# Block differences of h in the index stage's score buffers, spread over the second half of the token stage

## The chip, the cores and the metric

The kernel runs on one core of a Trainium2 chip. The metric is the device time of one execution in microseconds. Three runs of the kernel before took 2882.2, 2875.97 and 2873.57 us; the median is 2875.97 us. The profile shown here is of one more execution, which took 2868.78 us.

## The reference

One step of a one-layer streaming encoder: a normalised, modulated input `h` is projected by one wide matrix, and its columns feed a sparse attention with an indexer, a gated short convolution, and merge gates.

```python
h = rms_norm(x, norm_g) * (1.0 + scale[:, None, :]) + shift[:, None, :]
proj = h @ w_in                     # 9,000-odd columns, split into
(q, k, v, za, qi, ki, wi, u, bg, cg, zb, ga, gb) = jnp.split(...)
...
logits = einsum('bqhd,bsd->bqhs', qi, ki) * IDX_DIM ** -0.5
score  = einsum('bqh,bqhs->bqs', wi * IDX_HEADS ** -0.5, relu(logits))
_, idx = lax.top_k(score, 256)      # then attention over the gathered keys
...
y = x + gate * (merged @ w_out)
```

There are 2048 prompt tokens and 32 sample tokens, 1024 model channels, 8 index heads of 64 channels.

## The kernel before

**Number format.** Every large product is made of three fast matmuls: an operand is split into a high part (a cast) and a low part (operand minus high part), and high x high, low x high and high x low are added up in PSUM.

**Token stage** (lines 492 to 901). `h` is made tile by tile (`mk_h`, line 633): a tile of x is normalised, transposed on TensorE, scaled into `f`, split into `hhi` and `hlo`, and `f` is stored to the DRAM tensor `h_d` (line 649), channels by tokens. From it come the columns i0 and i1 (index queries and keys), k and v: for each tile of 128 tokens and each column group, 24 matmuls (`chunk`, lines 760 to 762) into one of 5 PSUM banks `pm`. The copies out of PSUM go into 5 buffers `sm`, are turned or normalised on VectorE and stored. The tokens are done in two halves (8 tiles, then 9 with the sample tokens). `tok_steps` (line 740) gives a list of steps for a half: in the second half steps 0 to 22 are i0 and i1 with the making of `h` for later pairs of tiles (steps 4, 9, 14), step 23 prepares weights, steps 24 to 32 are k, steps 33 to 41 are v.

**Block differences.** The next stage multiplies `h` by the feature weights with seven products of half-size blocks in place of eight. It needs four differences of the four blocks of `h` (two halves of the channels by two halves of the tokens); they are kept in the DRAM tensor `t_d`. For a chunk of 352 (or 336) tokens and a pair of channel tiles kt and kt+4, `sums_load` (line 659) loads two tiles x from `h_d` (line 662, both token halves in one tile), and `block_sums` (line 664) makes four subtractions on VectorE (line 671) and stores both tiles to `t_d` (line 673). There are 12 such differences: 3 chunks by 4 values of kt. Their tiles come from `xtile`, the four buffers of tag x in pool `xp`, which also hold the raw x of `mk_h`. In the list of steps, the load of a difference stands at step 15 and every fourth position after it, its subtractions three positions later, and the next load right behind those.

**Feature stage, pass 0** (from line 903). Its pools lie over the SBUF space of the token stage's pools: the tiles `ev` through which operands come in (7 buffers) begin where `xp` began; the weight tiles `wr` (line 925), `ws` and `wo` lie over the token stage's weights, and most of the operand tiles `bh` and `bl` over `hhi` and `hlo`. `b_piece` (line 966) loads four tiles `ev` (line 974) from `h_d` or `t_d`, splits each into `bh` (ScalarE, line 190) and `bl` (VectorE, line 191). Pass 0 needs 9 such pieces, 36 loads: three pieces of `h_d`, then six of `t_d`. `mm` (line 982) then makes 12 matmuls a piece (lines 988 to 990).

**Index stage.** Woven between the products run the index scores (`index_steps`, line 213): transposes (line 237), two matmuls per 512 (or 352) keys and head (lines 246 and 247), relu on ScalarE (line 248), scaled sum on VectorE into a score tile `sc` (lines 250 and 252; two buffers of 8 KB a partition in pool `ip`), then a bisection for the threshold. The first block is the sample's (block 16, 32 tokens), then 15, 14, ...

**Order.** A scheduler orders the instructions of each engine ahead of time from the order in which the code emits them, their priorities and its own estimates; it may bring index work forward. Loads and stores, but for a few, are issued from one queue, SyncE's (SP), in that order: a DMA that waits there holds all behind it. `tc.keep_in_program_order` fixes the order of the loads and subtractions of the differences among themselves.

Of the kernel before, what the change touches and what calls it, by code (L numbers as in the profile page):

```python
# [9 lines left out]
F32 = mybir.dt.float32  # L10
# [9 lines left out]
P = 128  # L20
D = 1024
KT = 8
SEQ = 2048
# [5 lines left out]
HT = NTOK // 2  # L29
# [35 lines left out]
TCOLS = _o  # L65


class Env:
    def __init__(self, **kw):
        self.__dict__.update(kw)  # L70
# [31 lines left out]

@with_exitstack
def body(ctx, tc, x_prompt, x_sample, cache_k, cache_v, cache_idx_k, state_conv, c_prompt, c_sample,
         w_ada, w_g, b_ada, norm_g, w_t, w_f, q_norm_g, k_norm_g, conv_w, w_q, rope, turns, ident_in, rows_in,
         y_p, y_s, k_p, v_p, ki_p, conv_p, k_s, v_s, ki_s, conv_s):
    nc = tc.nc
    V, S, G, T = nc.vector, nc.scalar, nc.gpsimd, nc.tensor
    load = nc.sync.dma_start
# [4 lines left out]
    def nm(s):  # L114
        uid[0] += 1
        return f"{s}_{uid[0]}"
# [35 lines left out]
    ident = cp.tile([P, P], F32, name="ident")  # L152
# [7 lines left out]
    heads = cp.tile([P, 8], F32, name="heads")  # L160
# [328 lines left out]
    ip = pix.enter_context(tc.tile_pool(name="ip", bufs=1))  # L489
# [17 lines left out]
    with ExitStack() as p1:  # L507
# [9 lines left out]
        def xtile():  # L517
            return xp.tile([P, D], F32, name=nm("x"), tag="x", bufs=4)
# [134 lines left out]
        halved = {}  # L653
# [3 lines left out]
            return x[:, :2 * tb].rearrange("p (h t) -> p h t", h=2), d.rearrange("p (h t) -> p h t", h=2)[:, :, c0:c0 + tb]  # L657

        def sums_load(ch, kt):
            xs = halved[ch, kt] = xtile(), xtile()  # L660
            for x, k in zip(xs, (kt, kt + 4)):
                tc.keep_in_program_order(load(*both(x, h_d[k], *CHUNKS[ch])))

        def block_sums(ch, kt):

            c0, tb = CHUNKS[ch]
            x1, x2 = halved.pop((ch, kt))
            a, b = slice(0, tb), slice(tb, 2 * tb)
            for o, p, q in ((x1[:, a], x1[:, b], x1[:, a]), (x1[:, b], x2[:, b], x1[:, b]),
                            (x2[:, b], x2[:, b], x1[:, a]), (x2[:, a], x2[:, a], x2[:, b])):  # L670
                tc.keep_in_program_order(V.tensor_tensor(o, p, q, ALU.subtract))
            for x, k in ((x1, kt), (x2, kt + 4)):
                store(*both(x, t_d[k], c0, tb)[::-1])
# [64 lines left out]
        def tok_steps(tiles, pairs, w0, p0, first):  # L738

            pend = []
            steps = []

            def flush():
                now = pend[:]
                pend.clear()
                for f in now:
                    f()

            def chunk(pi, ti):
                kind, cols = TOK[pi]
                hi, lo = wspl[w0 + pi]
                ncol = sum(w for _, w in cols)
                t, n, off = tiles[ti]
                r0 = t * P
                pm = acc()
                for kt in range(KT):
                    a, b_ = hhi[:, kt, off:off + n], hlo[:, kt, off:off + n]
                    T.matmul(pm[:n, :ncol], a, hi[:, kt, :ncol], start=(kt == 0), stop=False)  # L760
                    T.matmul(pm[:n, :ncol], a, lo[:, kt, :ncol], start=False, stop=False)
                    T.matmul(pm[:n, :ncol], b_, hi[:, kt, :ncol], start=False, stop=(kt == KT - 1))
                flush()
                if ti == 1 and pi > 1:
                    w_ahead(w0 + pi)
                if kind == "k":
                    sq = norm_stage1(pm, n)

                    def fin():
                        qn = norm_stage2(pm, sq, gk, t, n)  # L770
                        dst = (k_p[0, r0:r0 + n] if t < NB else k_s[0]).rearrange("t h d -> t (h d)")
                        store(dst, qn[:n, :256])
                        store(k_d[r0:r0 + n, :], qn[:n, :256])
                    pend.append(fin)
                elif kind == "v":
                    vs = small()
                    S.copy(vs[:n, :256], pm[:n, :256])
                    S.dma_start((v_p[0, r0:r0 + n] if t < NB else v_s[0]).rearrange("t h d -> t (h d)"), vs[:n, :256])
                    S.dma_start(v_d[r0:r0 + n, :], vs[:n, :256])
                elif kind == "i0":  # L780
                    vs = small()
                    S.copy(vs[:n, :264], pm[:n, :264])

                    def fin():
                        V.tensor_copy(wi[:n, t, :], vs[:n, 256:264])
                        rope_apply(vs[:n, :256].rearrange("p (h d) -> p h d", h=4), 4, 16, t, n)
                        store(qi_d[r0:r0 + n, 0:256], vs[:n, :256])
                    pend.append(fin)
                else:
                    vs = small()  # L790
                    S.copy(vs[:n, :320], pm[:n, :320])

                    def fin():
                        rope_apply(vs[:n, :320].rearrange("p (h d) -> p h d", h=5), 5, 16, t, n)
                        store(qi_d[r0:r0 + n, 256:512], vs[:n, :256])
                        store(ki_p[0, r0:r0 + n] if t < NB else ki_s[0], vs[:n, 256:320])
                        store(ki_d[r0:r0 + n, :], vs[:n, 256:320])
                        if t < NB:
                            pend.append(idx_key(env, kiT, r0, vs[:n, 256:320], n))
                        else:  # L800
                            pend.append(idx_key(env, kiS, PAST, vs[:n, 256:320], n))
                    pend.append(fin)

            def pair_ahead(i):
                if i + 2 < len(pairs):
                    mk_h(p0 + i + 2)
                if i == 1:
                    w_load(w0 + 2)

            for i, pr in enumerate(pairs):  # L810
                for pi in range(2):
                    for ti in range(2 * i, 2 * i + len(pr)):
                        steps.append((1.0, lambda pi=pi, ti=ti: chunk(pi, ti)))
                steps.append((0.3, lambda i=i: pair_ahead(i)))

            def third():
                w_split(w0 + 2)
                w_load(w0 + 3)

            steps.append((0.1, third))  # L820
            for pi in range(2, nw):
                for ti in range(len(tiles)):
                    steps.append((1.0, lambda pi=pi, ti=ti: chunk(pi, ti)))
            if first:
                for j in range(2):
                    at = len(steps) - (len(tiles) - 4 - 3 * j)
                    steps.insert(at, (0.3, lambda j=j: mk_h(p0 + len(pairs) + j)))
            else:
                at = 15
                for j in range(12):  # L830
                    ch, kt = j // 4, j % 4
                    steps.insert(at, (0.0, lambda ch=ch, kt=kt: sums_load(ch, kt)))
                    steps.insert(at + 3, (0.1, lambda ch=ch, kt=kt: block_sums(ch, kt)))
                    at += 4
            steps.append((0.1, flush))
            return steps

# [52 lines left out]
    with ExitStack() as p2:  # L890
# [183 lines left out]
        def turns_load(hf, ch):  # L1074

            c0, tb = CHUNKS[ch]
            turned[ch] = ev(), ev()
            for a, t in enumerate(turned[ch]):
                load(t[:, :tb], turns[a, :, hf * HT + c0:hf * HT + c0 + tb])

        def query(ct, f, hf, ch, uu, ps, second):

# [792 lines left out]
def _consts():  # L1875
    pos = np.concatenate([np.arange(SEQ), PAST + np.arange(NS)]).astype(np.float32)
    cols = []
    for rot in (32, 16):
        hf = rot // 2
        inv = np.float32(500000.0) ** (np.float32(-2.0) * np.arange(hf, dtype=np.float32) / np.float32(rot))  # L1880
        ang = (pos[:, None] * inv[None, :].astype(np.float32)).astype(np.float32).astype(np.float64)
        cols += [np.cos(ang), np.sin(ang)]
    table = np.concatenate(cols, axis=1).astype(np.float32)
    rows = np.zeros(32, np.float32)
    rows[0:ROUNDS + 1] = 0.5 ** np.arange(ROUNDS + 1)
    rows[16:24] = np.arange(1, 9)
    table = np.concatenate([table, np.zeros((17 * P - NTOK, 48), np.float32)]).reshape(17, P, 48).transpose(1, 0, 2).reshape(P, 17 * 48)
    turns = np.stack([np.tile(t.T, (8, 1)) for t in cols[:2]]).astype(np.float32)
    heads = np.kron(np.eye(8), np.ones((16, 1)))
    return {"rope": table, "turns": turns, "ident": np.concatenate([np.eye(P), heads], axis=1).astype(np.float32), "rows": rows}  # L1890


def _chunks(w):
# [59 lines left out]
```

## Time and profile before

| what | value |
|---|---|
| profiled execution, its own time | 2868.78 us |
| its span, first to last instruction | 2867.0 us |
| median of three runs | 2875.97 us |
| TensorE (PE) matmuls, busy | 2749.5 us, 18206 |
| VectorE (DVE) busy | 2193.7 us, 4549 instructions |
| ScalarE (ACT) busy | 1508.4 us, 2719 instructions |
| GpSimd (POOL) busy | 1049.3 us, 1430 instructions |
| mean granted TensorE clock | 0.984 |

The token stage's second half begins at about 150 us of the span; its last matmul starts at 270.99 us. The page of a profile lists busy time per engine, then the span in 40 slices of 71.7 us, in which each digit is a busy share (or the granted clock) in tenths. Other views used below are stages (busy time in chosen stretches, with the granted clock, the busy share of the DMA engines and GB/s behind it), groups of instructions by line and shape, the timeline of an engine or queue in order of time, and who waited for whom.

### The profile page before, as it was taken

To read this page: it belongs to the slowest core of one execution; us is meant where nothing else is said; L and a number is where in the kernel's file an instruction comes from. 1 tells how busy PE (TensorE), PEld (TensorE's weight loads), DVE (VectorE), ACT (ScalarE), POOL (GpSimd) and SP (SyncE) were. 2 spreads that over 40 slices of the span, in tenths; PEclk is the share of its full clock that TensorE was granted. 3 is DMA by queue.
4 is the path that set the end of the run, shared out by engine and by line. 5 is a ranking of instruction groups with operands and counts; after the bars stand their busy time and mean duration, and the time that the engine had idled before them with its cause. 6 is when DMAs were issued, how large, how long until landed. Compare 5 with 4: busy or idle time off the path is not lost. (4 is left out here: it accounts for less than half of the span.)

```text
span 2867.0 us, 51829 instructions
## 1 busy us (share of the span) xinstructions
PE 2749.5 (96%) x18206; PEld 2642.5 (92%) x18206; DVE 2193.7 (77%) x4549; ACT 1508.4 (53%) x2719; POOL 1049.3 (37%) x1430
## 2 busy tenths in 40 slices
PE   8998699999999989999999999999999999999998
PEld 6997399999999989999999999888999989999998
DVE  6665947477777789788887865888887768887988
ACT  4442635656665674434554432666666655454453
POOL 3331455456455334222342221467554430010100
PEclk9999799999999999999999999999999999999999
DMA  8547754544445476565676766567655459896785
GB/s 290 181 158 248 240 168 167 175 161 171 161 159 169 155 217 220 196 198 182 220 216 219 218 211 209 142 178 203 166 161 150 127 181 346 265 290 223 247 294 158
DMA packets 485841, 576.29 MB, mean 201 GB/s; under 512 B 179506, under 2 KB 375298, under 8 KB 484546
## 3 DMA queue, kind: packets, MB, share of 16 engines
q1 hardware_dynamic: 476706, 556.55, 61.8%
q0 software_dynamic: 4160, 12.06, 1.2%
q10 hardware_dynamic: 4704, 4.26, 0.5%
q8 instruction: 145, 2.38, 0.4%
q14 instruction: 126, 1.03, 0.1%
HBM read 379.83 MB, written 199.22 MB: 202 GB/s over the span
## 5 line engine op out<-in xcount | busy, mean ns | idle before, releaser
L988 PE MATMUL pm<-bh,wo 128*128 128x352 f32 (+1 forms) x2688 | 867.0, 324 | 13.1 <-DVE u L1087 8.4
L989 PE MATMUL pm<-bl,wo 128*128 128x352 f32 (+1 forms) x2688 | 866.3, 322 | 2.2 <-DVE bl L191 2.1
L990 PE MATMUL pm<-bh,wo 128*128 128x352 f32 (+1 forms) x2688 | 864.0, 323 | 0.4 <-POOL wo L191 0.4
L988 PEld LDWEIGHTS pm<-bh,wo 128*128 128x128 f32 x2688 | 508.1, 189 | 21.6 <-DVE u L1087 10.1
L989 PEld LDWEIGHTS pm<-bl,wo 128*128 128x128 f32 x2688 | 509.2, 189 | 9.4 <-DVE bl L191 3.5
L990 PEld LDWEIGHTS pm<-bh,wo 128*128 128x128 f32 x2688 | 507.9, 189 | 4.0 <-POOL wo L191 0.8
L191 POOL TENSOR_TENSOR wo<-wr,wo 128x512 fp32r<-128x512 f32 x160 | 232.2, 1452 | 614.3 <-ACT wo L190 597.2
L252 DVE SCALAR_TENSOR_TENSOR sc<-pi,wi,sc 128x512 f32<-128x512 f32 (+3 forms) x287 | 191.6, 670 | 68.1 <-ACT pi L248 64.2
L248 ACT ACTIVATE pi<-pi 128x512 f32<-128x512 f32 (+3 forms) x328 | 165.5, 517 | 143.3 <-PE pi L247 140.0
L1525 ACT CAST wh<-rw 128x1024 fp32r<-128x1024 f32 x128 | 134.2, 1053 | 167.9 <-PE ps L1700 77.6
L190 ACT CAST th<-pt 128x512 fp32r<-128x512 f32 (+1 forms) x288 | 154.1, 561 | 122.5 <-PE pt L1429 109.9
L1699 PE MATMUL ps<-xh,wh 128*128 128x384 f32 (+1 forms) x672 | 214.3, 321 | 2.0 <-ACT oa L1654 0.8
L1700 PE MATMUL ps<-xl,wh 128*128 128x384 f32 (+1 forms) x672 | 214.4, 320 | 0.0
L191 DVE TENSOR_TENSOR tl<-pt,th 128x512 fp32r<-128x512 f32 (+1 forms) x288 | 183.9, 655 | 37.9 <-ACT th L190 37.1
L1701 PE MATMUL ps<-xh,wl 128*128 128x384 f32 (+1 forms) x672 | 211.6, 320 | 0.5 <-DVE wl L1526 0.5
L1526 DVE TENSOR_TENSOR wl<-rw,wh 128x1024 fp32r<-128x1024 f32 x128 | 155.3, 1220 | 51.8 <-ACT wh L1525 51.8
L1408 ACT ACTIVATE s<-s,sc,rts 128x640 f32<-128x640 f32 (+15 forms) x128 | 166.0, 1298 | 49.6 <-DVE sc L1407 43.5
L1780 POOL DMA_DIRECT2D out_dram<-om x60 | 31.7, 534 | 389.9 <-DVE om L1778 389.9
L190 ACT CAST wo<-wr 128x512 fp32r<-128x512 f32 x160 | 98.3, 616 | 144.3 <-PE pm L989 114.4
L315 ACT ACTIVATE low<-sc,w 32x1056 f32<-32x1056 f32 (+14 forms) x105 | 136.6, 1301 | 62.7 <-DVE w L320 61.8
L1053 DVE TENSOR_TENSOR u<-u,pm 128x352 f32<-128x352 f32 (+1 forms) x240 | 122.2, 510 | 56.6 <-PE pm L990 54.9
L1437 PE MATMUL po<-th,vhi 128*128 128x256 f32 x544 | 158.9, 292 | 5.3 <-ACT th L190 3.0
(324 smaller groups left out, 7226.6 us busy)
## 6 DMA issues: line engine op xcount, KB each, us to landing
u<-u_d SPq DMA_DIRECT2D x128, 520.0 KB, 3.9
wr<-in_w_f_dram SPq DMA_DIRECT2D x96, 512.0 KB, 4.1
rw<-o_d SPq DMA_DIRECT2D x72, 512.0 KB, 5.0
u_d<-ev SPq DMA_DIRECT2D x192, 176.0 KB, 2.2
rw<-in_w_q_dram SPq DMA_DIRECT2D x56, 512.0 KB, 7.5
s_d<-ws SPq DMA_DIRECT2D x64, 256.0 KB, 2.8
wr<-s_d SPq DMA_DIRECT2D x32, 512.0 KB, 4.6
xa_d<-a SPq DMA_DIRECT2D x64, 256.0 KB, 3.4
```

The lines of the kernel that those rows point to most:

```text
L190: S.copy(hi, src)
L191: (eng or V).tensor_tensor(lo, src, hi.bitcast(F32), ALU.subtract)
L248: S.activation(pi[:n, :w], pi[:n, :w], AF.Relu)
L252: V.scalar_tensor_tensor(sc[:n, o:o + w], pi[:n, :w], wi[:n, b, h:h + 1], sc[:n, o:o + w], ALU.mult, ALU.add)
L988: T.matmul(ps[:, :tb], wh[:, kt, :], bh[:, kt, :tb], start=(first and kt == 0), stop=False, **more)
L989: T.matmul(ps[:, :tb], wh[:, kt, :], bl[:, kt, :tb], start=False, stop=False, **more)
L990: T.matmul(ps[:, :tb], wl[:, kt, :], bh[:, kt, :tb], start=False, stop=(kt == 3), **more)
L1408: S.activation(sm[:, :L], sm[:, :L], AF.Exp, bias=sc[:, 16 + i:17 + i], scale=r, accum_out=sc[:, 18 + i:19 + i])
L1437: T.matmul(po[:, 0:256], vh_, th[:, pc], start=(j == 0), stop=False)
L1699: T.matmul(ps[:, :tb], wh[:, kt, wc], xh[:, kt, :tb], start=(first and kt == 0), stop=False, **more)
L1700: T.matmul(ps[:, :tb], wh[:, kt, wc], xl[:, kt, :tb], start=False, stop=False, **more)
L1701: T.matmul(ps[:, :tb], wl[:, kt, wc], xh[:, kt, :tb], start=False, stop=(kt == 3), **more)
```

## The change

The twelve differences take their tiles from the two score buffers `sc` of the index stage (one 8 KB tile a difference, whose first two kilo-elements are the two x tiles), in place of the four x buffers. A table `SUMS_AT` puts them into the list of steps by the number of the original step: at its j-th entry the load of difference j stands first, and then the subtractions of difference j-1. So the first load stands behind step 1, the last behind step 32, and the last subtractions behind step 35 of 0 to 41. A load is always emitted one difference ahead. The input table `turns` is also renamed `rots`, with no other edit to it.

```diff
+SUMS_AT = (1, 4, 7, 10, 12, 15, 18, 20, 23, 26, 29, 32, 35)
...
         def sums_load(ch, kt):
-            xs = halved[ch, kt] = xtile(), xtile()
+            t = ip.tile([P, SEQ], F32, name=nm("hv"), tag="sc", bufs=2)
+            xs = halved[ch, kt] = t[:, 0:D], t[:, D:2 * D]
             for x, k in zip(xs, (kt, kt + 4)):
                 tc.keep_in_program_order(load(*both(x, h_d[k], *CHUNKS[ch])))
...
             else:
-                at = 15
-                for j in range(12):
-                    ch, kt = j // 4, j % 4
-                    steps.insert(at, (0.0, lambda ch=ch, kt=kt: sums_load(ch, kt)))
-                    steps.insert(at + 3, (0.1, lambda ch=ch, kt=kt: block_sums(ch, kt)))
-                    at += 4
+                at = {}
+                for j in range(13):
+                    at.setdefault(SUMS_AT[j], []).append(j)
+                put = []
+                for n, f in enumerate(steps):
+                    put.append(f)
+                    for j in at.get(n, ()):
+                        if j < 12:
+                            put.append((0.0, lambda c=divmod(j, 4): sums_load(*c)))
+                        if j:
+                            put.append((0.1, lambda c=divmod(j - 1, 4): block_sums(*c)))
+                steps = put
             steps.append((0.1, flush))
```

The scheduler turns this into another order on every engine. Two places follow, each before and after. In the rows a line number is that of the respective kernel (the changed one has lines 666, 677, 935, 984 for 662, 673, 925, 974, and 764 to 766, 998, 249 for 760 to 762, 988, 246); the number behind a name tells tiles apart; hv is the new tile.

First the SP queue where the differences end and the operands of pass 0 begin. Before (x holds the last difference, wr is a weight tile, ev an operand tile):

```order
L673 DMA t_d<-x_3647 256x1x336
L673 DMA t_d<-x_3648 256x1x336
L662 DMA x_3718<-h_d 128x2x336
L662 DMA x_3719<-h_d 128x2x336
L230 DMA qd_5710<-qi_d 128x4x64
L231 DMA qd_5710<-qi_d 128x4x64
L673 DMA t_d<-x_3718 256x1x336
L673 DMA t_d<-x_3719 256x1x336
L925 DMA wr_3902<-in_w_f_dram 128x1024
L925 DMA wr_3904<-in_w_f_dram 128x1024
L974 DMA ev_3912<-h_d 128x352
```

In the changed kernel the same place reads (sm_3599 is k of the last tile, so the v steps, whose stores go out from ScalarE's queue, are still to run):

```order
L666 DMA hv_3565<-h_d 128x2x336 x2
L677 DMA t_d<-hv_3427 256x1x336
L776 DMA out_dram<-sm_3599 32x256
L777 DMA k_d<-sm_3599 32x256
L984 DMA ev_3900<-h_d 128x352
L984 DMA ev_3904<-h_d 128x352
L677 DMA t_d<-hv_3565 256x1x336 x2
L984 DMA ev_3908<-h_d 128x352
L984 DMA ev_3912<-h_d 128x352
L984 DMA ev_3918<-h_d 128x352
L984 DMA ev_3922<-h_d 128x352
```

Before, the stores of the last seven of the twelve differences stand behind the last store of k; now all stores of differences but the last pair stand ahead of it. The weights wr come later than before: after all 12 operand loads from h_d and three from t_d.

Second, TensorE where the token stage's matmuls (pm from hhi and hlo) end. Before, the transposes and scores of block 16 follow (pi from kiS and qh or ql), 64 score matmuls in a row until the first product of pass 0:

```order
L762 MATMUL pm_3856<-wh_3202,hlo 32x256
L237 MATMUL pt_4124<-ident,qd_4118 128x32 x4
L246 MATMUL pi_4132<-kiS,qh_4122 32x352
L246 MATMUL pi_4158<-kiS,qh_4122 32x352
L247 MATMUL pi_4132<-kiS,ql_4123 32x352
L246 MATMUL pi_4137<-kiS,qh_4122 32x352
```

In the changed kernel products of pass 0 (pm from bh or bl and wo) stand right behind two score matmuls:

```order
L766 MATMUL pm_3844<-wh_3223,hlo 32x256
L240 MATMUL pt_4112<-ident,qd_4106 128x32 x4
L249 MATMUL pi_4120<-kiS,qh_4110 32x352
L249 MATMUL pi_4146<-kiS,qh_4110 32x352
L998 MATMUL pm_4082<-bh_3898,wo_3894 128x352
L999 MATMUL pm_4082<-bl_3899,wo_3894 128x352
```

The scores of block 16 are moved in among the products: 30 score matmuls stand ahead of the 61st product (92 before), 40 ahead of the 121st (99 before), and at the 600th product both orders have 112.

More of the change, by code (lines that the diff above doesn't have):

```diff
@@ L104, in body @@
 def body(ctx, tc, x_prompt, x_sample, cache_k, cache_v, cache_idx_k, state_conv, c_prompt, c_sample,
-         w_ada, w_g, b_ada, norm_g, w_t, w_f, q_norm_g, k_norm_g, conv_w, w_q, rope, turns, ident_in, rows_in,
+         w_ada, w_g, b_ada, norm_g, w_t, w_f, q_norm_g, k_norm_g, conv_w, w_q, rope, rots, ident_in, rows_in,
          y_p, y_s, k_p, v_p, ki_p, conv_p, k_s, v_s, ki_s, conv_s):
@@ L1078, in turns_load @@
             for a, t in enumerate(turned[ch]):
-                load(t[:, :tb], turns[a, :, hf * HT + c0:hf * HT + c0 + tb])
+                load(t[:, :tb], rots[a, :, hf * HT + c0:hf * HT + c0 + tb])
         def query(ct, f, hf, ch, uu, ps, second):
@@ L1887, in _consts @@
     table = np.concatenate([table, np.zeros((17 * P - NTOK, 48), np.float32)]).reshape(17, P, 48).transpose(1, 0, 2).reshape(P, 17 * 48)
-    turns = np.stack([np.tile(t.T, (8, 1)) for t in cols[:2]]).astype(np.float32)
+    rots = np.stack([np.tile(t.T, (8, 1)) for t in cols[:2]]).astype(np.float32)
     heads = np.kron(np.eye(8), np.ones((16, 1)))
-    return {"rope": table, "turns": turns, "ident": np.concatenate([np.eye(P), heads], axis=1).astype(np.float32), "rows": rows}
+    return {"rope": table, "rots": rots, "ident": np.concatenate([np.eye(P), heads], axis=1).astype(np.float32), "rows": rows}
 def _chunks(w):
```

## The prediction, made before the run

> **What bounds the kernel now.** I read the page first, then stages of the span, then the timelines around the stage that the diff touches. The page says TensorE:
>
> ```profile
> span 2867.0 us, 51829 instructions
> PE 2749.5 (96%) x18206; PEld 2642.5 (92%) x18206; DVE 2193.7 (77%) x4549; ACT 1508.4 (53%) x2719; POOL 1049.3 (37%) x1430
> PE   8998699999999989999999999999999999999998
> PEclk9999799999999999999999999999999999999999
> ```
>
> The reader is to see the fifth digit (287 to 358 us): TensorE busy 6 tenths, at 7 tenths of its clock. Nowhere else do both fall. The stages there (columns: length, busy us of PE, PEld, DVE, ACT, POOL, granted clock, DMA share, GB/s):
>
> ```profile
> 150.00:206.00 56.00, 53.52 (x394) 51.27 (x393) 37.31 (x119) 23.82 (x65) 24.89 (x46) 1.00 0.45 149
> 206.00:271.20 65.20, 63.04 (x530) 60.78 (x528) 38.90 (x148) 19.28 (x77) 14.39 (x26) 1.00 0.72 228
> 271.20:309.60 38.40, 20.13 (x66) 7.61 (x66) 23.71 (x48) 13.32 (x32) 0.00 (x0) 0.63 0.73 227
> 309.60:318.40 8.80, 4.87 (x13) 2.05 (x12) 7.03 (x16) 7.70 (x16) 3.94 (x8) 0.86 0.89 311
> 318.40:360.00 41.60, 28.53 (x106) 21.37 (x105) 41.04 (x74) 32.47 (x70) 25.12 (x16) 0.71 0.76 242
> 360.00:440.00 80.00, 77.95 (x475) 76.77 (x474) 35.75 (x65) 34.19 (x63) 42.33 (x39) 0.98 0.49 165
> 440.00:960.00 520.00, 512.70 (x3125) 500.70 (x3125) 369.59 (x640) 319.94 (x565) 283.93 (x236) 1.00 0.49 165
> ```
>
> The token stage's second half (the first two rows) keeps TensorE busy 116.6 of 121.2 us. Its matmuls end at 271.2, and the first product of pass 0 starts at 318.41. The timeline of the SP queue says why (start, us, instruction):
>
> ```profile
> 207.09 0.36 SPq L649 DMA_DIRECT2D h_d<-f  x1
> 207.55 1.30 SPq L662 DMA_DIRECT2D x<-h_d  x2
> ...
> 294.00 1.23 SPq L662 DMA_DIRECT2D x<-h_d  x2
> ...
> 299.32 2.86 SPq L673 DMA_DIRECT2D t_d<-x  x2
> 302.23 1.28 SPq L662 DMA_DIRECT2D x<-h_d  x2
> ...
> 307.42 2.60 SPq L673 DMA_DIRECT2D t_d<-x  x2
> 310.07 1.09 SPq L925 DMA_DIRECT2D wr<-in_w_f_dram  x2
> 312.38 3.17 SPq L974 DMA_DIRECT2D ev<-h_d  x7
> ```
>
> The twelve differences run one after another: load, four subtractions, two stores, and only then the next load. From the first load to the twelfth are (302.23 - 207.55) / 11 = 8.6 us each. The chain starts behind the last store of h and ends 39 us after the token matmuls; the operand loads ev, whose buffers lie over the x tiles, come behind it.
>
> **What those 89 us cost.** TensorE did some work in them, which now has to be done elsewhere, so I count it at full-clock spacing (0.16 us for 352 columns, 0.23 for 512, from the starts below). The first six rows group the matmuls from 271.2 to 360 by shape, the seventh is of 360 to 440:
>
> ```profile
> L246 PE MATMUL pi<-kiT,qh 128*128 128x512 f32 x23 | 12.6, 555 | 14.2 <-DVE sc L252 8.8 <-DVE w L319 2.8 <-DVE w L316 2.2
> L247 PE MATMUL pi<-kiT,ql 128*128 128x512 f32 x22 | 11.3, 532 | 3.6 <-DVE w L316 3.5
> L246 PE MATMUL pi<-kiS,qh 128*32 128x352 f32 x24 | 11.3, 478 | 8.8 <-DVE kiS L209 4.2 <-DVE sc L252 3.7 <-ACT qh L190 0.4
> L247 PE MATMUL pi<-kiS,ql 128*32 128x352 f32 x24 | 10.8, 468 | 7.5 <-DVE ql L191 7.5
> L988 PE MATMUL pm<-bh,wo 128*128 128x352 f32 x20 | 7.6, 378 | 0.0
> L988 PE MATMUL pm<-bh,wo 128*128 128x336 f32 x4 | 1.4, 358 | 0.0
> ...
> L246 PE MATMUL pi<-kiT,qh 128*128 128x512 f32 x10 | 4.0, 396 | 0.0
> ...
> 360.12 0.40 PE L247 MATMUL pi<-kiT,ql 128*128 128x512 f32 x1
> 360.35 0.40 PE L246 MATMUL pi<-kiT,qh 128*128 128x512 f32 x1
> 376.00 0.32 PE L990 MATMUL pm<-bh,wo 128*128 128x352 f32 x1
> 376.16 0.32 PE L988 MATMUL pm<-bh,wo 128*128 128x352 f32 x1
> ```
>
> From 271.2 to 360 stand 45 score matmuls of 512 columns, 48 of 352, 72 products (24 for each of lines 988 to 990) and some 16 transposes: 10.4 + 7.7 + 11.5 + 1.6 = 31.2 us of work in 88.8, a loss of 57.6. By 309.6 it was about 10.1 of 38.4 (loss 28.3); behind that 21.1 of 50.4 (loss 29.3). From 360 to 440, 475 matmuls, 20 of them scores (10 a line), make 77.3 of 80, a loss of 2.7. Together **60 us** that a perfect start would save. Behind 440 the rows give 512.7 of 520: nothing to gain.
>
> **The change part by part.**
>
> *Nothing is added or removed* in arithmetic: 24 loads, 48 subtractions, 24 stores before and after.
>
> *Earlier.* With the last subtractions put behind step 35 (third tile of v; a matmul takes 63.04 / 530 = 0.12 us there, 24 are 2.9 us, and the six tiles behind it some 17 us), the exposed part of the chain goes: it takes 28.3 us of loss with it. What is late next is the start of pass 0.
>
> *Its cover in the token stage.* About 24 subtractions now fall there that did not before (six of twelve differences ended by 268.8). Durations, with two rows for what such a subtraction can cost:
>
> ```profile
> L671 DVE TENSOR_TENSOR x<-x,x x24: 485/519/528, 214.4 to 308.4; 128x352 f32<-128x352 f32 x16, 128x336 f32<-128x336 f32 x8
> L191 DVE TENSOR_TENSOR bl<-ev,bh 128x352 fp32r<-128x352 f32 x24 | 19.8, 849 | 0.0
> L191 DVE TENSOR_TENSOR bl<-ev,bh 128x336 fp32r<-128x336 f32 x11 | 5.6, 530 | 0.0
> ```
>
> 24 x 0.52 = 12.5 us more for VectorE, which is busy 76.2 of 121.2 us there. The same kind of subtraction took 0.85 us on the mean between 318.4 and 360, where GpSimd was busy 25 of 41.6 us; at that price all 48 make 41 us in place of 25. The Trainium skill, SBUF — State Buffer, section "Who interferes with whom", says that a VectorE instruction with two SBUF inputs contends with a GpSimd one that reads SBUF and that the loser blocks fully; by it the early differences, which now run beside the lo splits of h on GpSimd, would cost up to the 0.85, so 16 us more. That speaks against the change; the 0.85 agrees, the 0.53 shows it doesn't hold always. Either way VectorE's work stays under 120 us only with 45 us of idle as cover, and the five PSUM banks (2.9 us of matmuls each) lie between it and TensorE. I take 2 us for the token stage's end (bounds: 2 us earlier, since fewer waits stand at its end, to 20 us later, all of the extra VectorE work on the path).
>
> *The start of pass 0.* Behind the token matmuls comes the weight wr, whose place was theirs: landing and cast.
>
> ```profile
> DMA to landing us min/median/max: 5.8/5.8/5.8
> L190 ACT CAST wo<-wr x2: 600/606/613, 315.4 to 330.7; 128x512 fp32r<-128x512 f32 x2
> L252 DVE SCALAR_TENSOR_TENSOR sc<-pi,wi,sc 32x352 f32<-32x352 f32 x21 | 11.9, 569 | 2.0 <-ACT pi L248 1.1
> ```
>
> That is 5.8 + 0.6 = 6.4 us, less the few score matmuls in it: 6 us lost. Until steady, the stage 318.4 to 360 was VectorE's: 41.04 of 41.6 us, 25.4 of it in 35 splits bl. In the changed order eight of the 36 splits can run before the token matmuls end (their tiles lie over memory long free); 28 remain, at 25.4/35 = 0.73 us 20.3 us, and 17 score sums of block 16 between them (0.57 us, 9.7) where block 15's larger ones and the bisection stood. 30 us, then, beside which TensorE has 120 products and 40 scores, 25.6 us of work, by the changed order. So the floor of the loss is about 6 us, the ceiling 6 plus the 22.3 that the old stage 318.4 to 360 lost (41.6 less 72 x 0.16 and 34 x 0.23). I take **16**, between the two, since the clock falls back in the 6 us gap (0.63 to 0.86 in the rows above wherever TensorE waits) and the pieces come one by one.
>
> *Sum.* 60.3 - 16 - 2 = 42 us, on the profiled execution's 2868.8 us: 2827. The median of the runs shown is 2876.0, 7.2 above the profiled one; the forecast for a median is **2835 us**, rounded up. Ends: floor 60 - 6 + 2 = 56 (2820), ceiling 60 - 28 - 5 = 27 (2849).
>
> *Score buffers.* The 8 KB tiles are idle then: the first score tile is taken by block 16, behind the token matmuls in the changed order. Two buffers, each reused every second difference: a load waits for stores of two differences ago.
>
> **The rivals.**
>
> 1. *Only the tail goes.* Pass 0's start stays as slow as before (loss 29.3 + 2.7), because VectorE and the operand loads set it. Gain 28.3 - 2 = 26: 2850. For it: VectorE full and DMA at 0.76 in that row. Against: the order puts 15 of 36 operand loads ahead of the weights and 59 score matmuls fewer into it.
>
> 2. *Slower: the SP queue.* A load of a difference waits in the queue for its buffer's stores, and a store for VectorE; behind them wait the stores that free `sm`, then ScalarE's copies, then the banks of TensorE. Such waits exist:
>
> ```profile
> SPq L673 <- DVE x L671: 11.2, 11, 2.4
> ACT sm L777 <- DMA x<-h_d: 7.4, 1, 7.4
> ```
>
> If each of the twelve round trips of 8.6 us were laid bare on TensorE, 103 us would come on top of 2835: 2938. It decides from 41 / 12 = 3.4 us laid bare per difference. Against it: six such trips ran from 207 to 269, and TensorE was busy 63.0 of 65.2 us beside them. The Trainium skill, DMA: Bandwidth & Descriptors, section "Anatomy of one DMA — SWDGE (gpsimd) path", says that a semaphore wait happens on the issuing sequencer before dispatch, and that most of a DMA's fixed 2 us is the receipt of its last write: the queue would be held for it at each reuse. Waits in SP's rows agree; what it costs TensorE is what the trace denies.
>
> 3. *The token stage becomes VectorE's.* The extra 20 us bound above come onto the path: 42 + 2 - 20 = 24 us gain, 2852.
>
> 4. *The change doesn't do what it says.* Were the loads from h_d still held until its last store at 207.09, twelve differences at half the round trip (two in flight), 4.3 us, would end at 259, before 271.2; the gain stays. If held and not overlapped, nothing changes: 2876.
>
> 5. *Given back later.* The scheduler's order differs on all engines to the end. Its one place with slack is the end of pass 0:
>
> ```profile
> 960.00:1060.00 100.00, 89.98 (x524) 85.30 (x523) 81.14 (x173) 66.45 (x135) 32.21 (x30) 0.97 0.63 189
> ```
>
> If index work, which loses its early start, were what ends there, up to all 42 us would be lost: 2876. Against: both orders have the same 112 scores at product 600, and VectorE is busy 370 of 520 us in between.
>
> **How the numbers follow.** Forecast 0.66, rival 1 0.15, rival 3 0.05, rival 4 0.03 (0.01 of it held but overlapped, which is faster still), rival 5 0.05, rival 2 0.06. A measurement of this kernel tells about 0.3% (8.6 us) from no change. Faster by more: 0.66 + 0.15 + 0.05 + 0.01 = 0.87; same: 0.02 + 0.05 = 0.07; slower: 0.06. The range takes the forecast's ends, rivals 1 and 3, and 6 us each way for runs and reordering: 2814 to 2858.
>
> **What would show it.** Right: the last store to t_d ahead of the last token matmul; that matmul within 5 us of 271; the first product 5 to 8 us behind it (47 before); steady at about 300 to 305 in place of 360; stages behind shifted by 40 us at unchanged length. Wrong: TensorE waits inside 150 to 271 (rival 2 or 3); more than 45 us from the last token matmul to steady products (rival 1); a lower TensorE share behind 440 than before (rival 5).

## The result, and the profile after

| kernel | median, us | runs, us | ratio to before |
|---|---|---|---|
| before | 2879.09 | 2873.57 to 2882.94 | |
| changed | 2836.52 | 2831.79 to 2843.1 | 0.9855 [0.9827, 0.9884] |

The median fell by 42.6 us, to within 2 us of the forecast of 2835. The profiled execution of the changed kernel took 2831.79 us, 37.0 less than that of before. Its page, engine totals and the slices of TensorE and its clock:

```profile
span 2829.9 us, 51791 instructions
PE 2730.2 (96%) x18206; PEld 2636.1 (93%) x18206; DVE 2203.2 (78%) x4549; ACT 1506.2 (53%) x2719; POOL 1030.5 (36%) x1430
...
PE   8998899999999999999999999899999999999998
...
PEclk9999899999999999999999999999999999999999
```

The matmul count is the same. The fifth digit (283 to 354 us) is 8 where it was 6, and no slice of the clock is below 8. The stages show what the digits don't: from 150 to 206 us, where the differences now run, TensorE's busy time fell from 53.52 to 50.42 us. The stages of the changed kernel (columns as before):

```profile
150.00:206.00 56.00, 50.42 (x363) 48.52 (x361) 44.03 (x124) 22.52 (x59) 25.57 (x40) 0.97 0.74 239
206.00:271.20 65.20, 62.65 (x511) 59.84 (x511) 42.19 (x165) 20.27 (x81) 17.14 (x32) 1.00 0.81 259
271.20:280.00 8.80, 6.31 (x57) 5.87 (x55) 3.53 (x8) 4.20 (x13) 0.00 (x0) 1.00 0.94 298
280.00:290.00 10.00, 2.98 (x9) 2.15 (x10) 3.91 (x9) 4.38 (x11) 2.16 (x2) 0.56 0.90 294
290.00:300.00 10.00, 7.54 (x42) 6.29 (x40) 10.00 (x13) 6.58 (x17) 7.93 (x6) 0.93 0.85 258
300.00:310.00 10.00, 8.93 (x35) 6.24 (x36) 9.79 (x17) 6.27 (x17) 6.22 (x5) 0.66 0.79 244
310.00:320.00 10.00, 10.00 (x64) 9.36 (x64) 7.65 (x12) 7.47 (x19) 4.98 (x5) 1.00 0.84 275
```

From 310 on TensorE is full (from 360 before). The timeline of the SP queue (start, us, instruction) at the end of the token stage, and that of TensorE behind it:

```profile
267.04 1.23 SPq L677 DMA_DIRECT2D t_d<-hv  x2
268.32 6.64 SPq L984 DMA_DIRECT2D ev<-h_d  x8
275.05 0.45 SPq L233 DMA_DIRECT2D qd<-qi_d  x1
...
277.38 2.46 SPq L984 DMA_DIRECT2D ev<-t_d  x3
281.64 0.98 SPq L935 DMA_DIRECT2D wr<-in_w_f_dram  x2
```

```profile
276.87 0.28 PE L766 MATMUL pm<-wh,hlo 128*32 128x256 f32 x1
277.08 0.43 PE L240 MATMUL pt<-ident,qd 32*128 32x32 f32 x4
284.92 0.80 PE L249 MATMUL pi<-kiS,qh 128*32 128x352 f32 x2 [7.41 <-ACT qh L193]
287.81 0.66 PE L998 MATMUL pm<-bh,wo 128*128 128x352 f32 x1 [2.10 <-ACT wo L193]
```

The last stores to t_d go out at 267 to 268, ahead of the last token matmul at 276.9 (271.0 before). The first product comes 10.7 us behind the last token matmul's end (47 before, 5 to 8 forecast): the weight wr is issued only at 281.64, behind 15 operand loads, eight of which take the queue 6.64 us to issue. In the last 1.8 us ahead of it (279.84 to 281.64) the queue issued nothing.

### The profile page after: what moved, and what is told of

It reads as the page before. It is cut to its first block, busy times and chain, and to the rows that moved or that the text cites. A ratio compares the mean times of both kernels' runs of the same rounds, so it can differ in the third digit from the quotient of the medians.

```text
span 2829.9 us, 51791 instructions
## 1 busy us (share of the span) xinstructions
PE 2730.2 (96%) x18206; PEld 2636.1 (93%) x18206; DVE 2203.2 (78%) x4549; ACT 1506.2 (53%) x2719; POOL 1030.5 (36%) x1430
## 5 line engine op out<-in xcount | busy, mean ns | idle before, releaser
L1418 ACT ACTIVATE s<-s,sc,rts 128x384 f32<-128x384 f32 (+15 forms) x128 | 166.2, 1298 | 48.3 <-DVE sc L1417 36.5
L193 ACT CAST wo<-wr 128x512 fp32r<-128x512 f32 x160 | 98.4, 615 | 140.9 <-PE pm L999 109.0
```

The lines of the kernel that those rows point to most:

```text
L193: S.copy(hi, src)
L1418: S.activation(sm[:, :L], sm[:, :L], AF.Exp, bias=sc[:, 16 + i:17 + i], scale=r, accum_out=sc[:, 18 + i:19 + i])
```

## The experiments

Theory: the differences were a serial chain that ended 39 us too late; its end, and so the operands from t_d, sets when TensorE is full again. Rivals: the buffers alone (operand tiles no longer wait for x tiles), the load ahead alone, and other bounds on the new start. A table of all runs (in the kernels' own profiled executions: last token matmul, issue of the last store to t_d or of the short group it is in, start of the first product, and the start of the first 10 us from which TensorE is at least 9.8 of 10 us busy for 20 us on end):

| run | median, us | ratio to before | token end | last t_d | first product | full from |
|---|---|---|---|---|---|---|
| before | 2879.1 | | 271.0 | 307.4 | 318.4 | 360 |
| changed | 2836.5 | 0.9855 [0.9827, 0.9884] | 276.9 | 267.0 | 287.8 | 310 |
| buf_only | 2866.6 | 0.9968 [0.9957, 0.9978] | 271.5 | 323.6 | 288.0 | 340 |
| place_only | 2837.7 | 0.9878 [0.9856, 0.9899] | 277.4 | 268.6 | 287.6 | 320 |
| not_ahead | 2844.7 | 0.9897 [0.9879, 0.9916] | 277.7 | 276.3 | 292.5 | 320 |
| no_diffs | 2822.4 | 0.9821 [0.9801, 0.9840] | 267.8 | none | 272.5 | 290 |
| start10 | 2850.9 | 0.9918 [0.9899, 0.9936] | 274.8 | 284.8 | 291.5 | 320 |
| later6 | 2846.5 | 0.9905 [0.9887, 0.9922] | 272.4 | 292.6 | 291.4 | 320 |
| wr_early | 2850.9 | 0.9915 [0.9897, 0.9933] | 277.2 | 269.7 | 288.2 | 330 |
| wr_early_start10 | 2859.5 | 0.9946 [0.9928, 0.9964] | 273.8 | 280.9 | 292.7 | 340 |
| no_subs | 2835.0 | 0.9857 [0.9838, 0.9877] | 275.6 | 262.2 | 281.6 | 300 |
| wr_pool | 2838.6 | 0.9864 [0.9845, 0.9883] | 277.3 | 269.2 | 291.5 | 320 |
| earlier0 | 2834.9 | 0.9856 [0.9836, 0.9875] | 280.7 | 255.0 | 285.3 | 300 |
| earlier0_wr | 2834.9 | 0.9855 [0.9831, 0.9880] | 279.2 | 254.1 | 285.3 | 300 |

Each ratio is against runs of the kernel before on the same chip, medians 2874 to 2879. Gains below are these differences of medians on one chip, and an interval of a ratio is 3 to 8 us to either side.

### Buffers or places

**buf_only**, the kernel before with only the buffers changed:

```diff
         def sums_load(ch, kt):
-            xs = halved[ch, kt] = xtile(), xtile()
+            t = ip.tile([P, SEQ], F32, name=nm("hv"), tag="sc", bufs=2)
+            xs = halved[ch, kt] = t[:, 0:D], t[:, D:2 * D]
```

> The kernel before with the differences in the score buffers; their places in the list of steps (15, then every second) and the load right behind the subtractions of the difference before stay. My theory: the exposed tail comes from the serial chain of 12 times 8.6 us that starts late, so it stays: the stores to t_d end some 30 us behind the last token matmul, and of the 43 us only the part that comes from operand tiles lying over the x buffers is gained (products of pass 0 can start beside the chain: about 20 us). Ratio to before 0.993. Rival A, the buffers are all of it (the operand loads no longer wait for the x tiles): 0.985, as the whole change. Rival B, the placement is all of it: 1.000.

It gained 8.2 us (2874.8 to 2866.6). The SP queue, and a stage of ten us:

```profile
207.82 1.30 SPq L663 DMA_DIRECT2D hv<-h_d  x2
...
313.39 1.61 SPq L663 DMA_DIRECT2D hv<-h_d  x2
```

```profile
310.00:320.00 10.00, 1.63 (x5) 0.55 (x6) 5.43 (x9) 0.92 (x3) 5.78 (x5) 0.63 0.83 276
```

The chain starts at 207.8 as before (207.55), so the buffers did not hold it up. The first product comes at 288.0, as in the changed kernel, and then TensorE runs dry: 1.63 of 10 us at 310 to 320, since the pieces read from t_d are not there. An early first product is worth little (8 us, not the 20 expected) where the later operands are late. Rival A falls.

**place_only**, the changed kernel with the x tiles of before:

```diff
         def sums_load(ch, kt):
-            t = ip.tile([P, SEQ], F32, name=nm("hv"), tag="sc", bufs=2)
-            xs = halved[ch, kt] = t[:, 0:D], t[:, D:2 * D]
+            xs = halved[ch, kt] = xtile(), xtile()
```

> The changed kernel with the differences in the four x tiles as before; places and the load a difference ahead as changed. The x tiles are shared with the raw x of the tiles still to be normalised until step 14. My theory: the placement carries the tail, so at least 30 of the 43 us: ratio to before 0.988, last store to t_d ahead of the last token matmul or within 5 us of it. Rival A (the buffers are all of it): 1.000. Rival B (the placement is all of it): 0.985.

It gained 37.1 us, and its interval overlaps that of the whole change. The first load goes out at 174.6 (161.2 changed), since the raw x still hold the tiles, but the last stores at 268.6 all the same. **The places, with the load a difference ahead, carry the gain; the buffers add 5.5 us by the medians, which these runs don't tell from nothing.** Before, the differences had been emitted from step 15 on, every second step; what made them late was the round trip of 8.6 us each once they had begun at 207.

### The load a difference ahead

**not_ahead** puts each load right in front of its own subtractions:

```diff
                     for j in at.get(n, ()):
-                        if j < 12:
-                            put.append((0.0, lambda c=divmod(j, 4): sums_load(*c)))
                         if j:
+                            put.append((0.0, lambda c=divmod(j - 1, 4): sums_load(*c)))
                             put.append((0.1, lambda c=divmod(j - 1, 4): block_sums(*c)))
```

> The changed kernel with each load put right ahead of its own subtractions, three steps later than changed; score buffers and the places of the subtractions as changed. My theory: steps are about 3 us, a load with its landing about 3 to 5, so VectorE waits longer inside the token stage (7 us of waits for loads become 30 to 50), but a difference has 9 us to itself and the two buffers let it run: within 10 us of the changed kernel, ratio to before 0.987. Rival: the load ahead is what breaks the chain: ratio 0.995 or worse, stores to t_d behind the last token matmul by over 20 us.

A gain of 30.1 us, 0.9897 against 0.987 expected and 0.995 of the rival. The last store goes out at 276.3 in place of 267.0, and the first product 4.7 us later than in the changed kernel. By the gains the load ahead is worth 12.5 of the 42.6 us; the earlier places bring the other 30.1 without it.

### What the differences still cost

**no_diffs** makes no differences, **no_subs** only their loads and stores:

```diff
-                for j in range(13):
+                for j in range(0):
...
-            src, k0, hf = ((h_d, 0, 0), (t_d, 4, 1), (t_d, 0, 0), (t_d, 0, 1), (h_d, 4, 0), (t_d, 4, 0), (h_d, 4, 1))[k]
+            src, k0, hf = ((h_d, 0, 0), (h_d, 4, 1), (h_d, 0, 0), (h_d, 0, 1), (h_d, 4, 0), (h_d, 4, 0), (h_d, 4, 1))[k]
```

```diff
-                tc.keep_in_program_order(V.tensor_tensor(o, p, q, ALU.subtract))
+                pass
```

> The changed kernel without the twelve differences: nothing is loaded for them, subtracted or stored, and the pieces that read t_d read h_d in its place, with as many loads. It gives the floor: all that the differences still cost after the change. My theory: the token stage's last matmul comes at 270 to 272 again (277 with them), the weight wr and its cast remain, so 6 to 9 us below the changed kernel: ratio to before 0.983. Rival: the changed kernel still hides a large price of the differences (VectorE beside GpSimd, traffic): 20 us or more below it, 0.978 or less.

> The changed kernel with the loads and stores of the differences but without their 48 subtractions, so that t_d holds copies of h. Without differences the last token matmul came at 267.8, with them at 276.9: 9 us that are either VectorE's or the transfers' and the queue's. Theory (VectorE's extra 25 us beside the making of h): last token matmul at 268 to 271, ratio to before 0.982 to 0.983. Rival (the stores and loads in the SP queue, and what waits behind them): 274 to 277, ratio 0.985.

no_diffs gained 52.4 us, 10 more than the change. Its last token matmul came at 267.8 and the first product 4.7 us behind it, with wr issued at 268.10. So the differences, as changed, still cost 9.1 us in the token stage (3.2 before) and 6 in the start of pass 0. no_subs divides the 9.1 us. The groups of subtractions in the changed kernel, 150 to 277 us:

```profile
L675 DVE TENSOR_TENSOR hv<-hv 128x352 f32<-128x352 f32 x32 | 16.7, 525 | 1.8 <-DMA hv<-h_d 1.3
...
L675 DVE TENSOR_TENSOR hv<-hv 128x336 f32<-128x336 f32 x16 | 8.0, 502 | 5.8 <-DMA hv<-h_d 5.7
```

Without these 24.7 us of work the token stage ended at 275.6, 1.3 us sooner. The other 7.8 us stayed, and they came with the loads and stores. (The subtractions without the transfers were not run.) Who TensorE waited for, 150 to 277, in the changed kernel, and then without differences (us, times, longest):

```profile
PE pt L645 <- DVE f L649: 3.5, 2, 2.3
PE pm L765 <- DVE wl L194: 3.3, 2, 2.2
PE pt L208 <- DVE f L649: 1.1, 1, 1.1
```

```profile
PE pm L765 <- DVE wl L194: 1.0, 1, 1.0
...
PE pt L645 <- DVE f L649: 0.4, 1, 0.4
```

It waits for the tiles f of h and for weights, 7.9 us in place of 1.4. VectorE itself waits for the buffers f until their store has landed; the waits of VectorE, first without differences, then as changed, then in no_subs:

```profile
DVE f L649 <- DMA h_d<-f: 3.0, 3, 1.8
```

```profile
DVE f L649 <- DMA h_d<-f: 5.6, 3, 2.4
```

```profile
DVE f L649 <- DMA h_d<-f: 9.3, 4, 3.2
```

The DMA issues, 150 to 215 us, have the landing of the small stores of h in their last column, without differences and as changed:

```profile
h_d<-f SPq DMA_DIRECT2D x4, 32.0 KB, 1.6
```

```profile
h_d<-f SPq DMA_DIRECT2D x4, 32.0 KB, 3.1
```

They land in twice the time, and the last store of h goes out at 214.2 (206.3 without differences, 207.1 before). The making of h is what the early transfers hold up, by queue or by DMA engines; these runs don't part the two.

no_subs was no faster than the changed kernel in the end, though its first product came 6.2 us sooner. By the last store of s_d, at the end of pass 0, 3.2 us of it were left (909.8 against 913.0), by the first weight of pass 2 none (1329.4 against 1329.0).

### Later

**start10** and **later6** are only other tables:

```diff
-SUMS_AT = (1, 4, 7, 10, 12, 15, 18, 20, 23, 26, 29, 32, 35)
+SUMS_AT = (10, 12, 14, 16, 18, 20, 22, 25, 27, 29, 31, 33, 35)
```

```diff
-SUMS_AT = (1, 4, 7, 10, 12, 15, 18, 20, 23, 26, 29, 32, 35)
+SUMS_AT = (7, 10, 13, 16, 18, 21, 24, 26, 29, 32, 35, 38, 41)
```

> The changed kernel with the differences put later and closer: first load behind step 10, one every second step, last subtractions behind step 35 as changed. The changed kernel lost 5.6 of the first 50 us of 150 to 200 (2.5 before), where the differences run beside the making of h. My theory: VectorE's extra work beside the making of h is what moved the token stage's end from 271 to 277; with the first subtractions behind step 12 the end comes at 272 to 274 and the last store to t_d still ahead of it, so 3 to 5 us below the changed kernel: ratio to before 0.983 to 0.984. Rival: the later 48 subtractions just make the loss elsewhere (the chain needs 8 us for each of 12 and does not fit into the 100 us left): as changed or slower, 0.986 to 0.990, last store behind the last token matmul.

> The changed kernel with all entries of the table moved by six steps (7 to 41 in place of 1 to 35). It lays part of the tail bare again. My theory: six steps are 17 us; the last store lands some 5 to 10 us behind the last token matmul, but the first pieces read only h_d, so of it only what the pieces of t_d then lack is lost, and the token stage gains 1 to 3 us: 0 to 8 us above the changed kernel, ratio to before 0.986 to 0.989. Rival: each exposed difference costs its full 8.6 us, three of them 26: 0.994.

Of the 42.6 us of gain 19.4 and 15.0 are gone: start10 went the way of its rival and beyond it (0.9918, rival 0.986 to 0.990), later6 lies between its theory (0.986 to 0.989) and its rival (0.994). The token stage did end sooner, at 274.8 and 272.4, as the theory said; but the last stores came at 284.8 and 292.6, 10 and 20 us behind it, and TensorE was full only from 320. Stages of start10:

```profile
300.00:310.00 10.00, 6.61 (x42) 5.07 (x40) 9.90 (x17) 6.37 (x16) 4.11 (x4) 1.00 0.97 284
310.00:320.00 10.00, 4.38 (x20) 1.78 (x20) 9.79 (x15) 7.45 (x19) 6.92 (x5) 0.83 0.74 237
```

VectorE is full there and TensorE starves: the last of the 36 splits bl of pass 0's operands starts at 325.7 (316.9 as changed). A closer chain does not go faster: from the first load at 186.4 to the last store are 98.4 us, 8.2 for each difference even with a load ahead. So a late difference costs not its 8.6 us each time, but a delay of the pieces that read it: 19.4 us for last stores 17.8 us later in start10, 15.0 for 25.6 in later6. The last store alone doesn't set the loss: in later6 it is the later one, but all 12 operand loads from h_d were issued by 276.6 (282.7 in start10), and the last split starts at 320.3.

### The weight load

**wr_early** fixes wr behind the eighth operand load; **wr_early_start10** adds the table of start10; **wr_pool** issues the first two wr from GpSimd's queue.

```diff
-        w_load(0)
-        w_piece(0, 0)
         b_piece(0, 0)
         b_piece(0, 1)
+        w_load(0)
+        w_piece(0, 0)
...
+                if n == 0:
+                    tc.keep_in_program_order(ins)
...
+                if k in (0, 1):
+                    tc.keep_in_program_order(ins)
```

```diff
-                load(r, w_f[cc].rearrange("p (k c) -> p k c", k=2))
+                (load if n else G.dma_start)(r, w_f[cc].rearrange("p (k c) -> p k c", k=2))
```

> The changed kernel with the first two weight loads wr fixed in the queue behind the eighth operand load (of the first two pieces, whose tiles lie over free memory) and ahead of the ninth, in place of behind the fifteenth. My theory: the first product came 10.7 us behind the last token matmul since wr was issued 4.6 us behind it, held by operand loads; now wr is issued at the last token matmul, the first product 6 to 7 us behind it, and 4 us are gained: ratio to before 0.984. Rival: the operand loads that now come later (nine to fifteen) are what the products then wait for, so it is the same or up to 8 us slower, 0.985 to 0.988.

> Both edits, the differences from step 10 on and the weight loads ahead of the ninth operand load. My theory: the two gains are at different places and add up: 7 to 9 us below the changed kernel, ratio to before 0.982 to 0.983, near the kernel without differences (0.982). Rival: with the differences later, the last stores to t_d meet the weight loads in the queue and hold them: no better than the better of the two.

> The changed kernel with the first two weight loads wr issued from GpSimd's queue in place of SP's; nothing else is fixed. GpSimd does nothing between 271 and 287 but wait for them. In the changed kernel wr was issued 4.7 us behind the last token matmul, behind operand loads. Theory: now it is issued within 1 us of it, lands 5 to 6 us later, and the first product starts 7 to 8 us behind the last token matmul (10.9 before): 3 us gained, ratio to before 0.984 to 0.985. Rival: the products then wait for the operands that share the DMA engines with it, and the start is no sooner to be steady: 0.985 to 0.987.

The theories of all three missed; wr_early_start10 gained 14.6 us, less than either of its edits alone (23.2 each). wr_early moved wr by only 0.8 us:

```profile
274.81 5.95 SPq L986 DMA_DIRECT2D ev<-h_d  x8
280.86 0.85 SPq L935 DMA_DIRECT2D wr<-in_w_f_dram  x2
...
295.04 1.98 SPq L986 DMA_DIRECT2D ev<-h_d  x4
297.10 2.70 SPq L986 DMA_DIRECT2D ev<-t_d  x4
```

The differences use the same call that fixes the order, so the operand loads now come behind all of theirs; they start at 274.81 (264.23 changed), and the operands of t_d at 297.1 (277.38 changed). By the gains it cost 19 us, with the first product hardly moved (288.2): again the later pieces came late, the last split at 331.3. So this run does not test what it was made for. wr_pool does: wr was issued at 278.25, and landed in 6.2 and 7.9 us (5.4 from SP at 281.64), but its cast ran no sooner (289.57, 287.14 as changed). ScalarE's timeline:

```profile
284.25 0.36 ACT L781 COPY sm<-pm 32x256 f32<-32x256 f32 x1 [2.66 <-DMA ev<-h_d]
...
287.08 1.11 ACT L193 CAST bh<-ev 128x352 fp32r<-128x352 f32 x2 [0.98 <-DMA ev<-t_d]
288.50 0.48 ACT L193 CAST bh<-ev 128x352 fp32r<-128x352 f32 x1 [0.31 <-DMA ev<-t_d]
...
289.57 0.62 ACT L193 CAST wo<-wr 128x512 fp32r<-128x512 f32 x1
```

In ScalarE's order casts of operands stand ahead of that of wr, and wait for operands to land. The first product came at 291.5, and the time did not change by what can be told (2838.6): 0.9864 lies in the rival's range.

### Sooner

**earlier0** begins as changed and ends seven steps sooner; **earlier0_wr** adds the edit of wr_pool.

```diff
-SUMS_AT = (1, 4, 7, 10, 12, 15, 18, 20, 23, 26, 29, 32, 35)
+SUMS_AT = (1, 3, 5, 7, 9, 11, 13, 15, 17, 19, 22, 25, 28)
```

> The changed kernel with the table (1, 3, 5, 7, 9, 11, 13, 15, 17, 19, 22, 25, 28): as soon as before, but closer, last subtractions seven steps (20 us) sooner. Moving the differences later cost 10 to 14 us against the changed kernel, where last stores and operand loads came 7 to 25 us later. Theory: what sets the time is when the last differences leave the queue and VectorE free for the first operands; seven steps sooner the operand loads start at about 245 to 250 (264 before), the weight wr is issued right at the last token matmul and the first product comes 5 us behind it: 5 us gained, ratio to before 0.983 to 0.984. Rival: the making of h shares VectorE with more of the subtractions, the token stage ends later than 277 by as much: 0.985 to 0.988.

> Both: the table of earlier0 and the first two weight loads from GpSimd's queue. Theory: the sooner table already issues the weights in time, so the second edit adds nothing, within 3 us of earlier0. Rival: the SP queue still holds them, and 3 us more are gained.

The last store came 12 us sooner (255.0), the first product 2.5 us sooner, and TensorE was full from 300. But the token stage ended 3.8 us later, as the rival said (280.7; 279.2 in earlier0_wr). TensorE's timeline in earlier0, its last token matmul and its first product:

```profile
280.70 0.28 PE L766 MATMUL pm<-wh,hlo 128*32 128x256 f32 x1
...
285.31 0.66 PE L998 MATMUL pm<-bh,wo 128*128 128x352 f32 x1 [0.23 <-ACT wo L193]
```

The weight wr was issued at 281.0, right behind that matmul's end, and the first product came 4.6 us behind the matmul, as the theory said. So the theory's start and the rival's late token stage both came, and the time is the same: 2834.9, and 2834.9 with both edits, which earlier0_wr's theory had right. What made the token stage later, VectorE's work or the transfers, these two runs don't part. The last store of s_d, at the end of pass 0, is at 908.3 (913.0 changed, 947.3 before), so 4.7 us were ahead there; the first weight of pass 2 is loaded at 1328.7 (1329.0 changed, 1366.5 before). They were given back between; by what was not tried. No version that makes the differences beats the changed kernel by more than the intervals.

One time in the traces orders the gains of all runs better than the first product or the last store does: the start of the last of the 36 splits bl that make pass 0's operands. It is 301.2 in no_diffs (gain 52.4 us), 312 to 319 in no_subs, both earlier0, wr_pool, the changed kernel and place_only (37 to 43), 320 to 321 in later6 and not_ahead (28 and 30), 325.7 in start10 and 331.3 in wr_early (23 each), 336.7 in wr_early_start10 (14.6), 339.3 in buf_only (8.2) and 360.4 before. That is a pattern; no run moves this split alone.

## Why the prediction was right, and where it was off

- **The tail** (28.3 us of loss till 309.6, all gone): right. The last store to t_d came ahead of the last token matmul; place_only, where it does so from the old tiles, gained 37.1 us, and start10 and later6, where it does not, lost 15 to 19 us of the gain. buf_only adds what the prediction did not say: with the tail left, an early start of pass 0 brings 8 us.
- **The token stage's end** (2 us later, bounds 2 sooner to 20 later): 5.9 us later, within the bounds. The size was off, and the reason. The prediction put the price on VectorE, at 0.52 to 0.85 us for a subtraction beside GpSimd. They took 0.525, and without them the stage ended 1.3 us sooner. Most of the price is the transfers': against no differences at all 7.8 of 9.1 us remained with loads and stores alone. A VectorE price beside GpSimd of 16 us, which the prediction weighed, did not come up: all 48 subtractions took 0.49 to 0.59 us (the last section shows where the price went).
- **The start of pass 0** (a loss of 16): 18.8. From 277.1 to 360 stand 328 products and 48 scores of 352 columns at 0.16 us, 12 of 512 at 0.23 and some 12 transposes at 0.1: 64.1 of 82.9 us. Of these rows the first and the first of the scores:

```profile
L998 PE MATMUL pm<-bh,wo 128*128 128x352 f32 x74 | 25.3, 344 | 2.2 <-ACT wo L193 2.1
...
L249 PE MATMUL pi<-kiS,qh 128*32 128x352 f32 x24 | 8.7, 369 | 10.8 <-ACT qh L193 7.4 <-DVE sc L255 2.9 <-DVE sc L253 0.4
```

  The gap to the first product was 10.7 us, not 6: the prediction let wr be issued when its place came free, but it stood behind 15 operand loads, as the part on the change had shown; in earlier0, where the queue did not hold it, the gap was 4.3 us. Some of it came back: behind 360 the changed kernel lost nothing till 440 (2.7 before).
- **The sum**: 60.3 - 18.8 - 5.9 = 35.6 us by what was measured for the terms, 37.0 between the profiled executions, 42.6 between the medians, 42 forecast. The terms missed by 6 us together, which the interval of the medians (33 to 50 us) does not tell. (The 5 us that the upper end takes for the token stage stand on no row; 5.9 came.) That the median came within 2 us of the forecast is luck in part: both terms were taken too small, and the medians differ by 5.6 us more than the profiled executions that the terms were read from.
- **The signs.** The last store came ahead of the last token matmul, as it was to. That matmul was 5.9 us late (within 5), the first product 10.7 us behind it (5 to 8), steady at 310 (300 to 305). TensorE was busy 3.5 us less between 150 and 271.2 than before: a small part of what rivals 2 and 3 said.
- **The rivals.** 1 (only the tail goes, 2850): no; TensorE was full 33 us behind the last token matmul, before 89. 2 (SP queue, 2938): such waits cost at most 7.8 / 12 = 0.65 us a difference against the 3.4 from which it would decide. 3 (VectorE, 20 us): not so, at 1.3 us by no_subs. 4 (does nothing): the first load went out at 161. 5 (given back later): not for the change, as the last store of s_d is 34.3 us ahead and the first weight of pass 2 37.5; but it is what became of the extra 4.7 us of earlier0.

## What to carry to other kernels

Work that a later stage reads and that is made in rounds of load, compute and store is placed by when its last round must land, and its length is rounds times round trip, however little its engine does: begin early enough, and one round ahead. Here, once it ended ahead of the stage that hides it, sooner bought nothing: that stage ended later, and what was still won by the end of pass 0 (4.7 us) was given back behind it. Last rounds 18 and 26 us later cost 19 and 15 us. An early first instruction of the next stage was worth little (8 us); ask when its last operand is ready.

## What the runs showed of the hardware

**Who pays where VectorE and GpSimd meet.** In the changed kernel's timelines the same pair of engines meets at two places. First the token stage, VectorE and then GpSimd:

```profile
221.32 2.20 DVE L675 TENSOR_TENSOR hv<-hv 128x352 f32<-128x352 f32 x4
```

```profile
221.56 0.37 POOL L203 COPY sm<-sm 128x64 f32<-128x64 f32 x1 [7.84 <-DVE sm L725]
221.87 0.62 POOL L204 COPY sm<-sm 128x64 f32<-128x64 f32 x1
...
226.99 0.23 POOL L204 COPY sm<-sm 128x64 f32<-128x64 f32 x1
```

Then the start of pass 0, again VectorE and GpSimd:

```profile
294.22 4.57 DVE L194 TENSOR_TENSOR bl<-ev,bh 128x352 fp32r<-128x352 f32 x4
...
302.63 0.50 DVE L194 TENSOR_TENSOR bl<-ev,bh 128x352 fp32r<-128x352 f32 x1
```

```profile
294.92 3.08 POOL L194 TENSOR_TENSOR wo<-ws,wo 128x512 fp32r<-128x512 f32 x2
303.70 1.28 POOL L194 TENSOR_TENSOR wo<-wr,wo 128x512 fp32r<-128x512 f32 x1 [5.69 <-ACT wo L193]
```

In the token stage four subtractions in a row take 0.55 us each, and GpSimd's copies beside them 0.62 in place of 0.23: GpSimd pays, and TensorE waits for such a copy once between 150 and 277 us, for 0.3 us. At the start of pass 0 the split takes 1.1 us while GpSimd works on the weights (1.54 us an instruction, 1.28 at 303.70) and 0.50 while it rests: VectorE pays the more, and it is the engine that is full there. The Trainium skill, SBUF — State Buffer, section "Who interferes with whom", says that a VectorE instruction with two SBUF inputs and a GpSimd one that reads SBUF exclude each other, and that the order of issue decides who waits. Both places agree that the two hold each other up; the order of issue no run here tests. The prediction had only counted VectorE as the one who pays. What the splits at the start of pass 0 lose by it no run took away.

**One queue's issue time.** Eight operand loads took SP 6.64 us to issue, 0.83 each (the row is in the first section), and the weight behind them went out 4.5 us after its place came free, the last token matmul's end at 277.15. Not all of that is issue time: in the last 1.8 us of it the queue issued nothing. wr_pool shows that this delay was not the last one: without it ScalarE's order came next.
